# Forming gated-unit and gate projections of a conformer block from seven block products instead of eight

## The chip, the cores and the metric

The kernel runs on one core of a Trainium2 chip. Of its engines TensorE (PE) multiplies matrices, VectorE (DVE), ScalarE (ACT) and GpSimd (POOL) work elementwise, and SyncE (SP) issues nearly all transfers. The metric is the device time of one execution in microseconds. Three executions of the kernel before took 1762.32 to 1763.79 us, with a median of 1763.37 us.

## The reference

One block over 1024 tokens of width 1024 in float32: a gated convolution branch and an attention branch, mixed by gates, then a feed-forward part with a short convolution. Cut to what matters here:

```
h = rms_norm(x, norm1_g)
z = h @ w_in
glu_in, q, k, v, gate_logits = split(z)

a = a_val * sigmoid(a_gate)                       # glu_in: 1024 + 1024 channels
a = causal_depthwise_conv(a, conv_w, conv_b)      # 31 taps for each channel
a = silu(rms_norm(a, conv_norm_g))
y_a = a @ w_conv_out

o = mix of three dilated causal window attentions over q, k, v (16 heads)
y_b = o @ w_attn_out

g = sigmoid(gate_logits + gate_b)                 # 1024 + 1024 channels
g_a, g_b = split(g)
x = x + (g_a * y_a + g_b * y_b) @ w_out

u = causal_depthwise_conv(rms_norm(x, norm2_g) @ w_up, ffn_conv_w, ffn_conv_b)   # 3 taps
x = x + (silu(u_gate) * u_val) @ w_down
```

The kernel merges the three attentions into one with a host-made mask for each head.

## The kernel before

**Numbers.** Every operand of a large matmul is split into a high and a low part (`split`, L76: ACT copies the high part into a rounded format, DVE subtracts it from the source), and a product is three matmuls: high by high, high by low, low by high. One matmul takes a 128x128 piece of weights or activations against 512 columns. A weight block of 128 output channels and 1024 inputs is a `[128, 1024]` tile: `stage` (L81) loads it into `raw`, and `wsplit` (L86) splits it into `whi` and `wlo`. Each of these three has four buffers.

**The order of the work.** The program is written as loops, and a planner orders each engine's instructions at build time by program order and by a timeline that it computes. Inside the `manual_schedule` blocks the order on ACT, DVE and PE is as written. The stages are:

1. *Start.* Eight token tiles of x are normalised and transposed into `hT`, which is high and low parts for token halves 0 and 1. The first gated-unit pair, channel block 0 of `a_val` with block 0 of `a_gate`, is computed in between (`first_pair`, L338).
2. *Gated units.* The other seven pairs: for each, 96 matmuls over the two weight blocks and the two token halves (`gemm_ch`, L115), a sigmoid on ACT and a product on DVE (L445) into `apad`, the convolution's input, which stays on the chip (ten buffers, used for the results too).
3. *Projections of q, k and v.* Six column groups by eight token tiles of 24 matmuls each (`gemm_tok`, L120). ACT and DVE normalise, transpose (on PE) and split the results, which go out to DRAM.
4. *The convolution* (`conv_branch`, L450) is 31 instructions on DVE for each of eight channel blocks (L458, L461), then squares on ACT and their sum on DVE (L469). It stands behind stage 3 in the program, and so it takes the time on DVE that stages 2 and 3 leave. PE sums the squares over channels (`pss`, L553), POOL takes the power, and PE spreads it over partitions (`psr`, L563). Then eight products on DVE (L568), silu on ACT (L569) and a transfer to DRAM (`da`, L570) end it.
5. *Side work.* `side_steps` (L178) is a generator of 48 uses of eight steps. A step is three matmuls of a gate projection (16 channel blocks by two token halves) or of `w_conv_out` (eight by two). `cover` (L542) takes `COVER[0]` = 24 steps ahead of `pss`, 8 steps between it and `psr`, and 20 steps behind the eight products. The last four gate blocks also ask for the convolution's results.
6. *Attention*, in a written order of 128 slots, eight a head (L654). In a slot PE computes scores for 128 queries (`score`, L581), DVE adds the mask and finds the minimum (L592), ACT takes the exponential, DVE and POOL normalise, and `BACK` = 5 slots later PE turns the result (`flip`, L603, matmuls of L607), ACT and DVE split it, and PE multiplies it by the values. `fill` (L639) takes `FILL[slot % 8]` steps of the side work in each slot, 17.5 a head. Attention's tiles lie on the memory of the convolution.
7. *The rest*: the gates are applied, `w_out`, the up projection and the down projection. Both of the last are already formed from seven block products; for the up projection `product` (L846), `up_sums` (L872) and `up_rest` (L1028) do it, and the token blocks for it are formed in `blocks`.

The lines that decide how the side work is spread:

```
FILL = (1.5, 3.4, 1.8, 1.9, 1.6, 3.0, 2.1, 2.2)
BACK = 5
SHARE = 0.6
COVER = (24, 8, 20)
```

Of the kernel before, what the change touches and what calls it, by code (L numbers as in the profile page):

```python
# [21 lines left out]
P = 128  # L22
# [12 lines left out]
FILL = (1.5, 3.4, 1.8, 1.9, 1.6, 3.0, 2.1, 2.2)  # L35
BACK = 5
SHARE = 0.6
COVER = (24, 8, 20)
# [14 lines left out]
def block_kernel(ctx: ExitStack, tc: tile.TileContext, x, g1, g2, pack, mask,  # L53
# [50 lines left out]

    def gemm_half(o, w, actT, half):

        hi, lo = w
        ah, al = actT[0][half], actT[1][half]
        for k in range(KT):
            pe.matmul(o, hi[:, k, :], ah[:, k, :], start=(k == 0), stop=False)  # L110
            pe.matmul(o, hi[:, k, :], al[:, k, :], start=False, stop=False)  # L111
            pe.matmul(o, lo[:, k, :], ah[:, k, :], start=False, stop=(k == KT - 1))  # L112
            yield

    def gemm_ch(ps, w, actT):  # L115
        for half in range(2):
            for _ in gemm_half(ps[:, half * 512 : half * 512 + 512], w, actT, half):
                pass

    def gemm_tok(ps, actT, wpieces, tt):  # L120

        half, c0 = tt // 4, (tt % 4) * P
        for k in range(KT):
            hi, lo = wpieces[k // 2]
            ah = actT[0][half][:, k, c0 : c0 + P]
            al = actT[1][half][:, k, c0 : c0 + P]
# [15 lines left out]
    da = dr.tile([P, KT, T], F32, name="da")  # L142
    dya = [dr.tile([P, T], F32, name=f"dya{i}") for i in range(8)]
# [34 lines left out]
    def side_steps(hT, da):  # L178
# [18 lines left out]
        def gate(c, half):  # L197
            def go(w):
                gp = bank_ps(f"gate_{c}_{half}")
                if c >= 12 and half == 1:  # L200
                    if not aT:
                        aT.extend(hb_tiles(hb1, "aT"))
                    ask_conv(0, 2 * (c - 12))
# [25 lines left out]
        for c in range(12):  # L229
            for half in range(2):  # L230
                gate(c, half)
        for half in range(2):
            for c in range(12, 16):
                gate(c, half)
        for c0 in (0, 4):
# [8 lines left out]
        for i, (_, n, go) in enumerate(uses):  # L244
# [7 lines left out]
            if n.startswith("co"):  # L252
                need = max(need, marks[(i - 32) // 4 % 2])
# [23 lines left out]
    p1a_cm = tc.tile_pool(name="ph1a", bufs=1, side="right")  # L277
    p1a = p1a_cm.__enter__()
    with tc.tile_pool(name="ph1", bufs=1) as p1:
        t4 = lambda name, dt=F32: p1a.tile([P, 1024], dt, tag="t4", bufs=4, name=name)  # L280
        g1r = p1.tile([1, D], F32, tag="csq", bufs=1, name="g1r")
        act.dma_start(g1r, g1.unsqueeze(0))
        xt = []
        for tt in range(8):
            xx = p1.tile([P, CW - 1 + T], F32, tag="apad", bufs=10, name=f"x_{tt}")[:, 0:T]
            sp.dma_start(xx, x[tt * P : (tt + 1) * P, :])
            xt.append(xx)
            if tt == 3:
                wfirst = [(c, n, stage(w_ch[c], n)) for c, n in ((8, "g0"), (0, "v0"))]
# [5 lines left out]
        hT = hb_tiles(hb1, "hT")  # L295

        glu0 = [big_ps("glugv_0"), None]
        third = big_ps("tp_2")
        gb1 = p1.tile([P, D], F32, tag="sqacc", bufs=1, name="gb1")
        xn = [t4(f"xs_{tt}") for tt in range(4)]  # L300
        st1 = p1.tile([P, 2, 8], F32, name="st1")
        tps = {}

        def squares(tt):
            if tt >= 4:
                xn.append(t4(f"xs_{tt}"))
# [9 lines left out]
        def turned(tt):  # L316
            for kk in range(2):
                ps = third[:, kk * 512 : kk * 512 + 512] if tt == 2 else bank_ps(f"tp_{tt}_{kk}")
# [5 lines left out]
        def part(tt, kk, a):  # L324
            half, c0 = tt // 4, (tt % 4) * P
            return hT[a][half][:, kk * 4 : kk * 4 + 4, c0 : c0 + P]
# [11 lines left out]
        def first_pair(half, ks, passes, which):  # L338
            o = glu0[half][:, which * 512 : which * 512 + 512]
            for wa, ha in passes:  # L340
                for k in ks:
                    pe.matmul(o, wfirst[which][wa][:, k, :], hT[ha][half][:, k, :],
                              start=(k == 0 and (wa, ha) == (0, 0)), stop=(k == 7 and (wa, ha) == (1, 0)))

        ENG = mybir.EngineType
        HH, HL, LH = ((0, 0),), ((0, 1),), ((1, 0),)
        with tc.manual_schedule(engines={ENG.Activation, ENG.DVE, ENG.PE}):
# [9 lines left out]
            for tt in range(4):  # L357
# [4 lines left out]
                if tt == 2:  # L362
# [4 lines left out]
            hl = [[wp.tile([P, 1024], F32R, tag=t, bufs=4, name=f"{t}_{n}") for t in ("whi", "wlo")]  # L367
                  for _, n, _ in wfirst]
            wraw = [r for _, _, r in wfirst]
            wfirst = [[t.rearrange("p (a b) -> p a b", a=KT) for t in w] for w in hl]  # L370
# [30 lines left out]
            squares(7)  # L401
            both(4, 0)
            scaled(6)
            spread1(7)
            both(5, 0)
            turned(6)
            both(4, 1)
            scaled(7)
            both(5, 1)
            first_pair(0, b, HL, 1)  # L410
            turned(7)
            first_pair(0, b, LH, 1)
            both(6, 0)
            both(7, 0)
            glu0[1] = big_ps("glugv_1")
            both(6, 1)
            ends = both(7, 1)
        for ks in (a, b):
            for which in range(2):
                first_pair(1, ks, HH + HL + LH, which)  # L420
        with tc.issue_after(ends[1].ins):
            dve.tensor_tensor(out=qkg, in0=pk[:, C_QG : C_QG + 1], in1=pk[:, C_KG : C_KG + 1], op=ALU.mult)
            dve.tensor_scalar(qkg, qkg, DH ** -0.5, None, op0=ALU.mult)
        with tc.issue_after(ends[0].ins), tc.issue_after(ends[1].ins):
            wsecond = [wpiece(w_ch[9], "g1"), wpiece(w_ch[1], "v1")]


        apad = []
        for c in range(8):
            a = p1.tile([P, CW - 1 + T], F32, tag="apad", bufs=10, name=f"apad_{c}")  # L430
            pool.memset(a[:, : CW - 1], 0.0)
            sg = t4(f"sg_{c}")
            if c == 0:
# [848 lines left out]
```

## Time and profile before

| what | value |
| --- | --- |
| median of three executions | 1763.37 us |
| profiled execution: span from first to last instruction | 1761.6 us |
| PE busy | 1749.1 us, 99% of the span |
| DVE busy | 1329.3 us, 75% |
| ACT busy | 771.7 us, 44% |
| moved by DMA | 272.79 MB, mean 155 GB/s |

The profiled execution has no time of its own beside its span; the span is 1.8 us under the median. A row of a group names the line, the engine, the operation, what is written and read, shapes and count, then its busy time and the mean duration of one. A mean duration counts the time in the pipeline, so that neighbours overlap; where a price is wanted, the distance from one start to the next is read. A row of the timeline or of the chain of waits begins with the start and the duration in us.

### The profile page before, as it was taken

How to read it: one execution, taken by the hardware profiler on the slowest of the kernel's cores; microseconds unless marked ns; L12 is line 12 of the kernel's file. 1: busy time of each engine (PE TensorE's matmuls, PEld its weight loads, DVE VectorE, ACT ScalarE, POOL GpSimd, SP SyncE). 2: the span in 40 equal slices, each digit the busy share in tenths (PEclk: the TensorE clock that was granted, in tenths of full speed). 3: DMA queues.
4: the chain of work that ended last, by engine and by line, in shares of the span. 5: the costliest groups of instructions: out<-in, count | busy, mean ns of one | idle time of the engine just before them, and what ended most of it. 6: DMA issues, size and time to landing. Idle time of an engine off the chain costs nothing.

```text
span 1761.6 us, 22662 instructions
## 1 busy us (share of the span) xinstructions
PE 1749.1 (99%) x8248; PEld 1454.3 (83%) x8248; DVE 1329.3 (75%) x1837; ACT 771.7 (44%) x1235; POOL 185.9 (11%) x193
## 2 busy tenths in 40 slices
PE   8999999999999999999999999999999999999999
PEld 6888888888888888888888888888888888888887
DVE  6999999999846666667655564687776777779863
ACT  6111132232256666667564343454544544534431
POOL 1000133034012222222210000000000000000000
PEclk9999999999999999999999999999999999999999
DMA  5111145344585655568446567532222222498851
GB/s 208 48 48 49 42 138 164 123 132 139 179 273 157 179 159 159 161 180 244 139 138 227 173 233 279 207 124 84 84 84 84 77 91 84 128 341 320 292 174 48
DMA packets 146530, 272.79 MB, mean 155 GB/s; under 512 B 11761, under 2 KB 61041, under 8 KB 146418
## 3 DMA queue, kind: packets, MB, share of 16 engines
q1 hardware_dynamic: 145264, 269.24, 47.2%
q10 hardware_dynamic: 1154, 2.10, 0.3%
q8 instruction: 65, 1.06, 0.2%
q14 instruction: 47, 0.39, 0.1%
HBM read 197.90 MB, written 73.40 MB: 154 GB/s over the span
## 4 chain that ended last, share of the span: by engine, by line
PE 93%; DMA 4%; DVE 1%; issue 1%; ACT 1%; SPq 0%; ACTq 0%; DVEq 0%
PE dx L1118 6%; PE xz L850 6%; PE xz L851 6%; PE xz L852 6%; PE qkv L129 5%; PE qkv L127 5%; PE qkv L128 5%; PE dy L1118 4%; PE pp L607 3%; PE gate L110 3%; PE gate L112 3%; PE gate L111 3%; PE y L850 2%; PE y L851 2%; PE y L852 2%; PE o L622 2%
## 5 line engine op out<-in xcount | busy, mean ns | idle before, releaser
L461 DVE SCALAR_TENSOR_TENSOR cacc<-apad,pk,cacc 128x1024 f32<-128x1024 f32 x240 | 299.7, 1288 | 0.7
L79 DVE TENSOR_TENSOR pl<-pp,ph 128x512 fp32r<-128x512 f32 x192 | 100.8, 553 | 88.1 <-ACT ph L78 87.9
L127 PE MATMUL qkv<-hi_qkv,hT 128*128 128x512 f32 x384 | 151.8, 396 | 0.0
L129 PE MATMUL qkv<-hi_qkv,hT 128*128 128x512 f32 x384 | 150.2, 391 | 0.0
L128 PE MATMUL qkv<-lo_qkv,hT 128*128 128x512 f32 x384 | 149.3, 389 | 0.0
L78 ACT ACTIVATE ph<-pp 128x512 fp32r<-128x512 f32 x192 | 87.1, 488 | 121.0 <-PE pp L607 120.3
L592 DVE CUSTOM_DVE_ANT_0 p<-s,m 128x128 f32<-128x128 f32 (+7 forms) x128 | 96.5, 754 | 53.3 <-PE s L588 41.4
L601 POOL TENSOR_SCALAR p<-p,st 128x128 f32<-128x128 f32 (+7 forms) x128 | 97.1, 758 | 315.7 <-DVE st L600 218.7
L1021 DVE SCALAR_TENSOR_TENSOR u<-u,pk 128x1023 f32<-128x1023 f32 x88 | 112.4, 1279 | 1.0 <-ACT u L1019 0.7
L103 POOL TENSOR_TENSOR rs<-ss,mhalf 128x8 f32<-128x8 f32 x32 | 75.0, 2348 | 337.6 <-DVE ss L102 337.6
L110 PE MATMUL gate<-hT,hi_gt 128*128 128x512 f32 x256 | 103.0, 402 | 0.0
L597 ACT ACTIVATE p<-p,st 128x128 f32<-128x128 f32 (+7 forms) x128 | 99.3, 775 | 5.5 <-DVE st L592 4.6
L111 PE MATMUL gate<-hT,hi_gt 128*128 128x512 f32 x256 | 100.3, 392 | 0.0
L112 PE MATMUL gate<-hT,lo_gt 128*128 128x512 f32 x256 | 100.1, 392 | 0.0
L129 PEld LDWEIGHTS qkv<-hi_qkv,hT 128*128 128x128 f32 x384 | 72.1, 188 | 15.3
L79 DVE TENSOR_TENSOR lo_uv<-raw_uv,hi_uv 128x1024 fp32r<-128x1024 f32 x20 | 24.5, 1226 | 79.5 <-ACT hi_uv L78 79.5
L128 PEld LDWEIGHTS qkv<-lo_qkv,hT 128*128 128x128 f32 x384 | 72.2, 188 | 14.3
L607 PE MATMUL pp<-ident,p 128*128 128x128 f32 x576 | 83.8, 272 | 0.0
L127 PEld LDWEIGHTS qkv<-hi_qkv,hT 128*128 128x128 f32 x384 | 72.2, 188 | 13.9
L607 PEld LDWEIGHTS pp<-ident,p 128*128 128x128 f32 x576 | 70.1, 140 | 15.3
L621 PE MATMUL o<-ph,v 128*128 128x512 f32 x192 | 74.8, 393 | 0.7 <-DVE op L633 0.7
L850 PE MATMUL xz<-blk_t,hi_s3g 128*128 128x512 f32 x176 | 68.6, 390 | 0.7 <-ACT xc L995 0.7
(309 smaller groups left out, 4638.8 us busy)
## 6 DMA issues: line engine op xcount, KB each, us to landing
wr<-w_down SPq DMA_DIRECT2D x45, 512.0 KB, 5.5
gr<-dff SPq DMA_DIRECT2D x62, 256.0 KB, 5.2
raw_qkv<-w_qkv SPq DMA_DIRECT2D x24, 512.0 KB, 3.8
dff<-u SPq DMA_DIRECT2D x22, 512.0 KB, 2.6
raw_uv<-w_up SPq DMA_DIRECT2D x21, 512.0 KB, 3.2
raw_ug<-w_up SPq DMA_DIRECT2D x20, 512.0 KB, 3.2
dv<-v SPq DMA_DIRECT2D x16, 512.0 KB, 3.2
raw_gt<-w_ch SPq DMA_DIRECT2D x16, 512.0 KB, 5.2
```

The source lines that it names most:

```text
L110: pe.matmul(o, hi[:, k, :], ah[:, k, :], start=(k == 0), stop=False)
L111: pe.matmul(o, hi[:, k, :], al[:, k, :], start=False, stop=False)
L112: pe.matmul(o, lo[:, k, :], ah[:, k, :], start=False, stop=(k == KT - 1))
L127: pe.matmul(ps, ah, hi[:, k % 2, :], start=(k == 0), stop=False)
L128: pe.matmul(ps, ah, lo[:, k % 2, :], start=False, stop=False)
L129: pe.matmul(ps, al, hi[:, k % 2, :], start=False, stop=(k == KT - 1))
L461: dve.scalar_tensor_tensor(out=acc, in0=a[:, j : j + T], scalar=w(j), in1=acc, op0=ALU.mult, op1=ALU.add)
L607: pe.transpose(pp[:, qb * P : (qb + 1) * P], pts[qb][:, kt * P : (kt + 1) * P], ident)
L850: pe.matmul(o, wh[:, k, :], bh[:, k, :], start=(start and k == 0), stop=False, skip_group_check=not start)
L851: pe.matmul(o, wh[:, k, :], bl[:, k, :], start=False, stop=False, skip_group_check=not start)
L852: end = pe.matmul(o, wl[:, k, :], bh[:, k, :], start=False, stop=(k == 3), skip_group_check=not start)
L1118: pe.matmul(banks[n], a[:, c], b[:, d], start=(start and i == 0 and m == 0), stop=(stop and i == nf - 1 and m == 2), skip_group_check=True)
```

## The change

For a pair of weight blocks, call the halves of the first a11, a12 (inputs 0 to 511, 512 to 1023) and those of the second a21, a22, and call the blocks of the activations b11, b21 (token half 0) and b12, b22 (token half 1). The two outputs for two token halves are eight block products of 12 matmuls. The change forms them from seven, with these sums:

```
s1 = a21 + a22   s2 = s1 - a11   s3 = a11 - a21   s4 = a12 - s2
t1 = b12 - b11   t2 = b22 - b12 + b11   t3 = b22 - b12   t4 = b21 - t2
```

- Pairs 0 and 1 of the gated unit stay plain and are computed at the start, half by half (`first_pair`). Their results go to DRAM (`dain`).
- Behind them DVE and ACT form and split t1 to t4, each 128 x 2048. They lie in a pool `phT` that lives until the last pair; b12 is parked in DRAM (`db12`) and fetched again, because its memory holds the pairs' outputs (`uring`).
- Pairs 2 to 7 of the gated unit, then gate blocks 0 and 1 with their partners 8 and 9, come from seven products (`pair_weights`, `pair_first`, `pair_sums`, `pair_rest`). The gated units go to DRAM, the gate logits too.
- The convolution reads its input from DRAM into two `apad` buffers. Its results stay on the chip: channel blocks 1 and 2 in two `cacc` buffers, 0 (by way of DRAM) and 3 to 7 in a pool `phc`, which lies behind `ph1`.
- The side work has 40 uses (12 gate blocks by two halves, then `w_conv_out`). `COVER[0]` is 48, and `FILL` is 12.4 steps a head.

The diff, cut:

```diff
-FILL = (1.5, 3.4, 1.8, 1.9, 1.6, 3.0, 2.1, 2.2)
+FILL = (1.1, 2.4, 1.3, 1.35, 1.15, 2.1, 1.5, 1.5)
-COVER = (24, 8, 20)
+COVER = (48, 8, 20)
+GATES = 2
+FAR = 3
...
-        for c in range(12):
+        left_over = [c for c in range(16) if c % 8 >= GATES]
+        turn = left_over[-4:]
+        for c in left_over[:-4]:
             for half in range(2):
                 gate(c, half)
...
+        def differ(tt):
+            c = slice((tt % 4) * P, (tt % 4) * P + P)
+            if "t1" not in plain:
+                plain["t1"] = p0.tile([P, 4, 512], F32, tag="xa", name="t1_sum")
+            act.activation(plain["t1"][:, :, c], tps[tt, 0], AF.Copy)
+            dve.tensor_tensor(out=plain["t3"][:, :, c], in0=tps[tt, 1], in1=plain["t1"][:, :, c], op=ALU.subtract)
...
+        pairs = [("u", c, w_ch[c], w_ch[8 + c]) for c in range(2, 8)]
+        pairs += [("t", c, w_ch[16 + c], w_ch[24 + c]) for c in range(GATES)]
...
+        def pair_first(xz, w):
+            for i, o in enumerate(xz):
+                b = [h0[a][:, 4 * i : 4 * i + 4] for a in range(2)]
+                product(o, four(w[0])[:, 4 * i : 4 * i + 4], four(w[1])[:, 4 * i : 4 * i + 4], *b, True)
...
+        def pair_sums(i, v):
...
+            add_(s1, a21, a22, ALU.add)
+            add_(s2, s1, a11, ALU.subtract)
+            sw = wsplit(s, f"{n}s12_{c}")
+            add_(a21, a11, a21, ALU.subtract)
+            gw = wsplit(g, f"{n}s3g_{c}")
+            add_(a12, a12, s2, ALU.subtract)
+            return [four(t) for t in sw], [four(t) for t in gw], [four(t) for t in wsplit(a12, f"{n}s4_{c}")]
...
+        spill(db12, upper[0])
+
+        def glu_end(c, half):
+            sg = cst.tile([P, 512], F32, tag="f2", bufs=2, name=f"sg_{c}_{half}")
+            act.activation(sg, glu[c, half][:, 0:512], AF.Sigmoid)
+            dve.tensor_tensor(out=sg, in0=glu[c, half][:, 512:1024], in1=sg, op=ALU.mult)
+            sp.dma_start(dain[c][:, half * 512 : half * 512 + 512], sg)
...
+        def form(n):
+            forms[n] = tform(n)
+            split(forms[n][:, 0], forms[n][:, 1], plain[n])
+
+        for n, k in (("t2", 0), ("t4", 4)):
+            dve.tensor_tensor(out=plain[n], in0=h0[0][:, k : k + 4].bitcast(F32),
+                              in1=h0[1][:, k : k + 4].bitcast(F32), op=add)
+        dve.tensor_tensor(out=plain["t1"], in0=plain["t1"], in1=plain["t2"], op=sub)
+        form("t1")
+        dve.tensor_tensor(out=plain["t2"], in0=plain["t3"], in1=plain["t2"], op=add)
+        form("t3")
+        form("t2")
+        dve.tensor_tensor(out=plain["t4"], in0=plain["t4"], in1=plain["t2"], op=sub)
+        form("t4")
...
+            put(uv[:, t0], X, 0)
+            dve.tensor_tensor(out=uv[:, t0], in0=Z, in1=uv[:, t0], op=add)
+            product(X, sh[:, 4:8], sl[:, 4:8], *fb["t2"], False)
+            put(uv[:, t1], X, 0)
+            product(Y, sh[:, 0:4], sl[:, 0:4], *fb["t1"], True)
+            put(p5, Y, 1)
+            product(X, gh[:, 0:4], gl[:, 0:4], *fb["t3"], False)
+            dve.tensor_tensor(out=ug[:, t1], in0=X, in1=p5, op=add)
+            product(Y, *s4, *fb["b22"], False)
+            dve.tensor_tensor(out=uv[:, t1], in0=Y, in1=uv[:, t1], op=add)
+            product(X, gh[:, 4:8], gl[:, 4:8], *fb["t4"], False)
+            put(ug[:, t0], X, 1)
+            if kind == "u":
+                act.activation(ug, ug, AF.Sigmoid)
+                dve.tensor_tensor(out=uv, in0=uv, in1=ug, op=ALU.mult)
+                sp.dma_start(dain[c], uv)
...
+        upper[0] = hb1.tile([P, 2, 4, 512], F32R, tag="hb01", name="b12_again")
+        fetch(upper[0], db12)
...
+                a = p1.tile([P, CW - 1 + T], F32, tag="apad", bufs=2, name=f"apad_{c}")
+                pool.memset(a[:, : CW - 1], 0.0)
+                sp.dma_start(a[:, CW - 1 :], dain[c])
+                if c < FAR:
+                    acc = p1.tile([P, T], F32, tag="cacc", bufs=2, name=f"cacc_{c}")
+                else:
+                    acc = pc.tile([P, T], F32, name=f"cn_{c}")
...
+                if c < FAR - 2:
+                    sp.dma_start(dacc[c], acc)
+                    acc = pc.tile([P, T], F32, name=f"cn_{c}")
+                    sp.dma_start(acc, dacc[c])
+                cn.append(acc)
```

More of the change, by code (lines that the diff above doesn't have):

```diff
@@ L410, in block_kernel @@
-            first_pair(0, b, HL, 1)
+            differ(5)
             turned(7)
-            first_pair(0, b, LH, 1)
+            glu[1, 0] = big_ps("glugv_10")
+            for which in range(2):
+                first_pair(0, (*a, *b), HH + HL + LH, which, 1)
             both(6, 0)
             both(7, 0)
-            glu0[1] = big_ps("glugv_1")
             both(6, 1)
[L417 to L420, printed above, removed]
```

236 lines of the change are left out of this document (153 added, 83 removed).

## The prediction

> **What bounds the kernel now.** I read the page first (busy shares, then the 40 slices), then the chain of waits, then windows and timelines round the place where the convolution ends.
>
> ```profile
> span 1761.6 us, 22662 instructions
> PE 1749.1 (99%) x8248; PEld 1454.3 (83%) x8248; DVE 1329.3 (75%) x1837; ACT 771.7 (44%) x1235; POOL 185.9 (11%) x193
> ...
> PE   8999999999999999999999999999999999999999
> ...
> DVE  6999999999846666667655564687776777779863
> ...
> PEclk9999999999999999999999999999999999999999
> ...
> L461 DVE SCALAR_TENSOR_TENSOR cacc<-apad,pk,cacc 128x1024 f32<-128x1024 f32 x240 | 299.7, 1288 | 0.7
> ```
>
> PE is busy in every slice, at the full granted clock: the end is set by the number of matmuls, so fewer of them is worth something. But the DVE row is also full, from slice 2 to slice 10 (44 to 440 us). What fills it is the convolution of L461, 300 us of work that yields to everything else. So in the first 480 us two engines are full, and a change that unloads the one and loads the other has to be counted on both.
>
> The price of a matmul is not its 390 ns mean but its distance to the next, which the chain of waits shows; the last two rows are the same point of two neighbouring column blocks of the up projection, which already forms a pair from seven products:
>
> ```profile
> 1719.91 5.44 PE dy L1118 x24
> ...
> 1299.07 0.45 PE xz L852 x2
> 1318.11 0.45 PE xz L852 x2
> ```
>
> 5.44 / 24 = 0.2267 us; 84 matmuls a pair times 0.2267 is 19.04, which is what the two rows are apart. A seven-product pair costs PE its matmuls and no wait there.
>
> The two ends of the convolution stage, PE's rows first, then DVE's, then the windows (columns: busy us of PE, PEld, DVE, ACT, POOL; clock; DMA):
>
> ```profile
> 470.45 0.39 PE L110 MATMUL gate<-hT,hi_gt 128*128 128x512 f32 x1
> ...
> 486.77 1.84 PE L553 MATMUL pss<-ones,sqacc 128*128 128x1 f32 x16
> ...
> 521.21 0.60 PE L607 MATMUL pp<-ident,p 128*128 128x128 f32 x4
> ```
>
> ```profile
> 480.61 1.23 DVE L469 TENSOR_TENSOR sqacc<-sqacc,csq 128x1024 f32<-128x1024 f32 x1 [1.19 <-ACT csq L468]
> ...
> 497.23 9.17 DVE L568 TENSOR_TENSOR cacc<-cacc,sqacc 128x1024 f32<-128x1024 f32 x8
> 513.06 0.29 DVE L592 CUSTOM_DVE_ANT_0 p<-s,m 128x128 f32<-128x128 f32 x1 [6.66 <-DMA da<-cacc]
> ```
>
> ```profile
> 0.00:44.00 44.00, 38.44 (x175) 30.07 (x176) 30.35 (x45) 26.77 (x42) 6.95 (x24) 1.00 0.55 209
> 44.00:482.00 438.00, 438.00 (x1994) 362.36 (x1993) 425.60 (x448) 102.54 (x140) 75.02 (x32) 1.00 0.34 106
> 482.00:513.00 31.00, 30.86 (x154) 25.81 (x152) 14.79 (x23) 14.71 (x18) 1.64 (x1) 1.00 1.03 315
> ...
> 550.00:600.00 50.00, 50.00 (x276) 42.62 (x276) 32.60 (x82) 30.80 (x71) 12.24 (x17) 1.00 0.56 158
> ```
>
> The last addition of squares ends at 481.84. PE left the projections at 470.45, covers with 24 gate steps (24 x 3 x 0.2267 = 16.3 us) and asks for the sum at 486.77: DVE is 5 us early. From there to the first flip of attention (521.21) PE has gate steps to do. The balance is a matter of 5 us; this is the place to watch.
>
> **The change, part by part.**
>
> *Matmuls.* Eight pairs go from 96 to 84: 96 fewer, 96 x 0.2267 = 21.8 us of PE. Nothing else on PE changes in number. Without any new idle time: 1763.4 - 21.8 = 1741.6 (span 1761.6, so 1.8 us lie around it). This is the floor.
>
> *DVE work ahead of the convolution's end.* Prices from DVE's timeline of the up projection, as distances between starts:
>
> ```profile
> 1313.90 1.22 DVE L79 TENSOR_TENSOR lo_s3g<-raw_ug,hi_s3g 128x1024 fp32r<-128x1024 f32 x1
> 1315.03 1.22 DVE L1025 TENSOR_TENSOR u<-u 128x1024 f32<-128x1024 f32 x1
> 1316.16 0.69 DVE L877 TENSOR_TENSOR s<-raw_ug 128x512 f32<-128x512 f32 x1
> 1316.77 1.28 DVE L1021 SCALAR_TENSOR_TENSOR u<-u,pk 128x1023 f32<-128x1023 f32 x1
> ```
>
> 1.13 us for 1024 columns, 0.60 for 512. A 2048-column addition is not in the trace: 1.13 + 2 x 0.53 = 2.2 at least, four times 0.60 = 2.4 at most; I take 2.2, since the step from 512 to 1024 shows the fixed part paid once.
> - A gated-unit pair: low halves of three 1024-wide weights and one 512 (3 x 1.13 + 0.60), four weight sums (2.4), three block sums (1.8), the gating product (1.13): 9.3. Before: two low halves and the product, 3.4. Six pairs: +35.6.
> - A gate pair: the same without the product, 8.2. Two: +16.4. The splits that they take out of the gate steps lay behind, since 48 cover steps ask for five weights where 24 asked for four: +1.2.
> - Token blocks: five additions and four low halves of 2048 columns, 9 x 2.2 = 19.8, and four 512-wide differences, 2.4: +22.2.
> - The two plain pairs cost what pairs 0 and 1 cost before.
>
> Together +75.4 us. The convolution cannot end before all of it is done, because it takes what DVE has left. DVE had 30.35 + 425.60 = 456.0 us busy and 26 idle up to 482; now 531.4 busy. Of the 26, some 15 belong to the first loads and to waits that a later filler cannot use; all 26 and 3 more (the first conv input now goes out to DRAM and back) is the other end. End of the convolution: 546 to 560; I take 553, the middle, as the idle rows do not say which of them go.
>
> *PE up to the first flip.* 521.2, plus 21.8 (96 more matmuls stand ahead of the projections: 192 + 8 x 84 against 768), plus 16.3 (24 more cover steps), less 2.0 (the first five slots fill 7.3 steps instead of 10.2): 557.3 if PE never waits. So DVE gets 71 us later and PE 36.
>
> *From the conv's end to the first flip.* Before: 34.4 us from the sum (486.77) to the flip (521.21), which PE filled; inside it the eight products end at 506.4, 19.6 after the sum, and the first score row waits 6.66 us for a normalised conv tile to leave, since it lies on that memory. Now the results lie in a pool of their own and the buffers that the convolution frees at its end come first in memory, where the early score tiles fall. The bounds: 12 (scores go into the gaps ahead of the products; the copies are done 10.5 after the sum) and 34.4. I take 18, nearer to the end of the products, since attention's first five slots need no flip and two score tiles in PSUM are all PE can run ahead. First flip 553 + 18 = 571; PE idle 571 - 557.3 = 14.
>
> The Trainium skill, "TensorE: Matmul & The Clock Gate", Part 1 (the HAM clock gate), says that after an idle window of about 3.4 us PE falls to half its clock and needs as long to come back. By that an idle stretch of 14 us would add up to about 1.7 us, an estimate from that page. This trace cannot settle it: its granted clock is full in all 40 slices, and it has no idle stretch so long.
>
> *Hidden parts.* ACT's extra casts and copies: ACT is busy 102.54 of 438 us in that window. The conv inputs through DRAM (8 x 0.5 MB out and in), the parked block (2 MB each way) and one result (0.5 MB each way) are 13.6 MB, 27 GB/s over 500 us at a DMA share of 0.34; SP's queue waits for the parked block behind the last pair's writes, but it is wanted only by the fifth token tile, 4 x 24 x 0.2267 = 21.8 us into the projections. Without that cover its 2 MB at the 315 GB/s of the 482 to 513 window cost 7 us. A wait inside the pair stage (a low half behind a conv instruction, 1.28 each) costs nothing while PE would idle later anyway; else 8 x 1.28 = 10 us. I take 0.5.
>
> *Attention with less fill.* Two heads, by the chain:
>
> ```profile
> 531.94 0.87 PE pp L607 x8
> ...
> 581.60 0.87 PE pp L607 x8
> ```
>
> 49.66 us. Fill falls from 17.5 to 12.4 steps a head, so 5.1 x 0.68 = 3.5 us a head go elsewhere: 42.7 for two. DVE has 32.60 and ACT 30.80 busy per 50 us, so 76% and 72% of the shorter time; with five slots between score and flip I expect little waiting: 0 to 10 us, I take 2 (nearest to the present rows, where PE is busy 50.00 of 50).
>
> Sum: 1763.4 - 21.8 + 14 + 2 + 0.5 = **1758** us.
>
> **The rivals.**
> - *Nearly all of the gain stays.* The conv ends at 546 and the scores slip in at 12: flip at 558, idle 1. 1763.4 - 21.8 + 1 + 1 = 1744. For it: DVE's idle time is waste that a longer queue could use. Against: it needs both low ends.
> - *DVE takes it all back (slower).* Place: PE's wait for the conv's sum and the tail behind it. If the conv ends at 556 or later and the tail stays as it is (34.4), the flip comes at 590: idle 33, 1763.4 - 21.8 + 33 + 1 = 1776. It decides from a first flip at 557.3 + 21.8 = 579 on. For it: +71 against +36 is the firmest count here, and the present tail is a measured row. Against: part of the tail was PE's own steps.
> - *Attention starves.* If a head cannot go below 23 us where PE needs 21.4, 16 x 1.6 = 26 us come on top of the idle 14: about 1782. DVE at 76% with in-order queues speaks for it, the five slots against.
> - *It doesn't do what it says*: pairs that wait as above, on a PE that is not idle later: 1763.4 - 21.8 + 10 + 3 = 1755, no longer apart from the forecast.
>
> **How the numbers follow.** Forecast (1749 to 1766) 0.45, of it 0.25 below and 0.20 within the 0.2% (3.5 us: 1759.8 to 1766.9) that a measurement of this kernel can tell from no change; nearly all stays 0.22; DVE takes it back 0.26; starving 0.07. The pair-wait case lies inside the first. Faster 0.25 + 0.22 = 0.47, same 0.20, slower 0.33. The range, 1744 to 1779, reaches from the first rival's number to just past the second's, leaving out the starving case and the ends. The forecast's own range is 1749 to 1766.
>
> **What would show it.** Pairs about 19.04 us apart between the plain pairs and the projections: the matmul part is right. DVE busy about 531 us up to the last addition of squares, and that addition between 546 and 560: the DVE count is right. PE's idle time gathered in one or two gaps between 525 and 575, released by the conv's sum, by a score tile or by a conv result's DMA: the idle term; its size against 14 decides between forecast and rivals. Heads 21.4 us apart: attention is not starved. The forecast is wrong if PE shows no idle stretch of over 5 us there, or one of over 25.

## The result, and the profile after

The kernel after takes 1783.34 us (median of 4 executions, 1780.02 to 1784.36) against 1763.58 us before (1762.32 to 1763.86): a ratio of 1.0109, 95% interval 1.0095 to 1.0123. It is slower by 1.1%, where 1758 was forecast, and 4 us above the top of the range. The rival "DVE takes it all back" is what happened.

The page, the rows that answer to those of before:

```profile
span 1781.2 us, 22699 instructions
PE 1740.7 (98%) x8152; PEld 1442.4 (81%) x8152; DVE 1394.6 (78%) x1919; ACT 809.0 (45%) x1280; POOL 185.5 (10%) x193
...
PE   7999999999996999999999999999999999999999
...
DVE  8999999999996677787764564687777777779863
...
PEclk9999999999998999999999999999999999999999
...
L628 DVE SCALAR_TENSOR_TENSOR cn<-apad,pk,cn 128x1024 f32<-128x1024 f32 x150 | 188.5, 1285 | 0.3
```

PE executes 8152 matmuls instead of 8248: the 96 are gone. But its row has a 6 in slice 13 (534 to 579 us), and its clock an 8 there. DVE's full stretch now ends two slices later than before. The waits of PE, longest first, say what PE stood for there:

```profile
PE pss L723 <- DVE sqacc L635: 14.5, 1, 14.5
PE qt L666 <- DVE qn L658: 5.5, 2, 4.2
PE tp L353 <- DVE sums L379: 2.8, 1, 2.8
```

And windows of the same kernel, of which the first overlaps the others (columns: length; busy us and instructions of PE, PEld, DVE, ACT, POOL; clock; DMA share; GB/s):

```profile
0.00:559.00 559.00, 527.36 (x2359) 431.29 (x2359) 533.66 (x588) 181.22 (x252) 79.64 (x56) 0.98 0.44 144
...
0.00:44.00 44.00, 34.35 (x142) 25.66 (x143) 35.40 (x50) 27.21 (x44) 7.30 (x16) 0.96 0.58 225
44.00:219.00 175.00, 174.08 (x767) 143.54 (x766) 167.33 (x168) 65.41 (x79) 0.30 (x3) 1.00 0.28 95
219.00:260.00 41.00, 36.78 (x156) 30.10 (x156) 39.32 (x43) 7.06 (x11) 9.69 (x5) 0.92 0.46 167
...
544.00:559.00 15.00, 0.50 (x5) 0.32 (x3) 13.46 (x12) 2.78 (x4) 0.00 (x0) 0.68 0.18 62
559.00:594.00 35.00, 34.69 (x156) 29.18 (x157) 16.06 (x34) 16.76 (x24) 3.78 (x5) 0.89 0.41 153
594.00:963.00 369.00, 366.90 (x2036) 311.47 (x2035) 262.03 (x647) 254.14 (x556) 96.85 (x124) 1.00 0.63 180
```

From 44 to 219 us, where the pairs are, PE works 174.08 of 175 us: the pairs themselves hardly wait. From 544 to 559 it does next to nothing (0.50 us), while DVE, busy 13.46 of 15, finishes the convolution. Then it works without a pause up to the first flip, 34.69 of 35 us, but at a clock of 0.89. These are the two ends of the stage, PE's timeline and DVE's:

```profile
544.17 0.28 PE L758 MATMUL s<-kl,q 128*128 128x128 f32 x1
558.95 3.58 PE L723 MATMUL pss<-ones,sqacc 128*128 128x1 f32 x16 [14.50 <-DVE sqacc L635]
562.38 0.77 PE L116 MATMUL gate<-hT,hi_gt 128*128 128x512 f32 x1
...
566.37 0.40 PE L116 MATMUL gate<-hT,hi_gt 128*128 128x512 f32 x1
...
569.81 1.31 PE L733 MATMUL psr<-dg,ones 128*128 128x128 f32 x10
```

```profile
557.67 1.23 DVE L635 TENSOR_TENSOR sqacc<-sqacc,apad 128x1024 f32<-128x1024 f32 x1 [1.18 <-ACT apad L634]
...
576.16 0.69 DVE L735 COPY sqacc<-psr 128x512 f32<-128x512 f32 x1 [4.37 <-PE psr L733]
576.88 1.23 DVE L738 TENSOR_TENSOR cn<-cn,sqacc 128x1024 f32<-128x1024 f32 x1
...
580.30 5.76 DVE L738 TENSOR_TENSOR cn<-cn,sqacc 128x1024 f32<-128x1024 f32 x5
585.97 0.29 DVE L762 CUSTOM_DVE_ANT_0 p<-s,m 128x128 f32<-128x128 f32 x1
```

The last addition of squares ends at 558.90 (before: 481.84), 77.1 us later. The first flip comes in the chain of waits of this kernel as follows, and two rows of the same form two heads apart stand behind it:

```profile
593.95 0.44 PE pp L777 x4
...
645.80 0.92 PE pp L777 x8
...
689.18 0.87 PE pp L777 x8
```

(PE's first flip starts at 593.8, 72.6 us later than before.) Behind it two heads take 43.38 us; before, 49.66. So up to the first flip the kernel loses 72.6 us, and behind it it gains 53.0, which is the fill moved forward and not a gain in work; the span is 19.6 longer.

### The profile page after: what moved, and what is told of

It is laid out like the page before. It is cut to its first block, busy times and chain, and to the rows that moved or that the text cites. A ratio compares the mean times of both kernels' runs of the same rounds, so it can differ in the third digit from the quotient of the medians.

```text
span 1781.2 us, 22699 instructions
## 1 busy us (share of the span) xinstructions
PE 1740.7 (98%) x8152; PEld 1442.4 (81%) x8152; DVE 1394.6 (78%) x1919; ACT 809.0 (45%) x1280; POOL 185.5 (10%) x193
## 4 chain that ended last, share of the span: by engine, by line
PE 88%; DVE 7%; ACT 2%; DMA 1%; issue 1%; POOL 0%; SPq 0%; DVEq 0%; ACTq 0%; POOLq 0%
PE dx L1278 6%; PE xz L124 6%; PE xz L126 6%; PE xz L125 6%; PE dy L1278 5%; PE qkv L140 3%; PE qkv L139 3%; PE qkv L141 3%; PE pp L777 3%; DVE cn L628 3%; PE gate L116 2%; PE y L126 2%; PE y L125 2%; PE y L124 2%; PE gate L117 2%; PE gate L118 2%
## 5 line engine op out<-in xcount | busy, mean ns | idle before, releaser
L628 DVE SCALAR_TENSOR_TENSOR cn<-apad,pk,cn 128x1024 f32<-128x1024 f32 x150 | 188.5, 1285 | 0.3
L762 DVE CUSTOM_DVE_ANT_0 p<-s,m 128x128 f32<-128x128 f32 (+7 forms) x128 | 96.4, 753 | 27.5 <-PE s L758 19.6
L628 DVE SCALAR_TENSOR_TENSOR cacc<-apad,pk,cacc 128x1024 f32<-128x1024 f32 x90 | 113.9, 1284 | 0.2
L81 DVE TENSOR_TENSOR lo_uv<-raw_uv,hi_uv 128x1024 fp32r<-128x1024 f32 x26 | 31.9, 1226 | 81.0 <-ACT hi_uv L80 80.4
L140 PE MATMUL qkv<-lo_qkv,hT 128*128 128x512 f32 x192 | 74.8, 391 | 0.9 <-DVE lo_qkv L81 0.9
L141 PE MATMUL qkv<-hi_qkv,hT 128*128 128x512 f32 x192 | 75.0, 391 | 0.0
L139 PE MATMUL qkv<-hi_qkv,hT 128*128 128x512 f32 x192 | 74.7, 395 | 0.0
L124 PE MATMUL xz<-blk_t,hi_s3g 128*128 128x512 f32 x176 | 68.6, 390 | 0.7 <-ACT xc L1155 0.7
L124 PE MATMUL xz<-h2left,hi_uv 128*128 128x512 f32 x176 | 68.6, 390 | 0.0
L125 PE MATMUL xz<-blk_t,hi_s3g 128*128 128x512 f32 x176 | 68.5, 389 | 0.0
L126 PE MATMUL xz<-h2left,lo_uv 128*128 128x512 f32 x176 | 68.5, 389 | 0.0
L125 PE MATMUL xz<-h2left,hi_uv 128*128 128x512 f32 x176 | 68.5, 389 | 0.0
L126 PE MATMUL xz<-blk_t,lo_s3g 128*128 128x512 f32 x176 | 68.5, 389 | 0.0
```

What stands on the lines that cost most here:

```text
L81: dve.tensor_tensor(out=lo, in0=src, in1=hi.bitcast(F32), op=ALU.subtract)
L124: pe.matmul(o, wh[:, k, :], bh[:, k, :], start=(start and k == 0), stop=False, skip_group_check=not start)
L125: pe.matmul(o, wh[:, k, :], bl[:, k, :], start=False, stop=False, skip_group_check=not start)
L126: end = pe.matmul(o, wl[:, k, :], bh[:, k, :], start=False, stop=(k == 3), skip_group_check=not start)
L628: dve.scalar_tensor_tensor(out=acc, in0=a[:, j : j + T], scalar=w(j), in1=acc, op0=ALU.mult, op1=ALU.add)
```

## The experiments

The theory after the result: the time follows the end of the convolution on DVE one to one, and what PE saves or loses ahead of it counts for nothing (A). The rivals: PE's own losses ahead of the reduction (B), the slots of work behind the reduction, attention, or the placing of a few additions. "Flip" is the first `pp`; all in us:

| run | median | ratio to before, 95% interval | last add ends | PE waits there | flip | median less last add |
| --- | --- | --- | --- | --- | --- | --- |
| before | 1763.58 | | 481.8 | 0 | 521.2 | 1281.7 |
| after | 1783.34 | 1.0095 to 1.0123 | 558.9 | 14.5 | 593.8 | 1224.4 |
| tap30 | 1775.45 | 1.0048 to 1.0078 | 551.0 | 11.9 | 585.8 | 1224.5 |
| start | 1780.86 | 1.0080 to 1.0114 | 555.6 | 20.5 | 590.6 | 1225.3 |
| tail | 1864.03 | 1.0546 to 1.0578 | 644.1 | 102.7 | 675.3 | 1219.9 |
| tail2 | 1778.76 | 1.0076 to 1.0106 | 556.5 | 9.1 | 588.4 | 1222.3 |
| cover80 | 1774.89 | 1.0045 to 1.0075 | 562.1 | 0 | 597.8 | 1212.8 |
| pool | 1789.82 | 1.0137 to 1.0167 | 563.1 | 7.9 | 599.0 | 1226.7 |
| pool_start | 1787.17 | 1.0122 to 1.0156 | 561.7 | 6.6 | 597.3 | 1225.5 |
| gates0 | 1779.55 | 1.0076 to 1.0106 | 548.3 | 4.8 | 583.4 | 1231.3 |
| best8 | 1772.96 | 1.0036 to 1.0064 | 557.4 | 6.1 | 594.1 | 1215.6 |
| best6 | 1766.86 | 1.0013 to 1.0031 | 547.2 | 0 | 582.9 | 1219.7 |
| before33 | 1780.75 | 1.0083 to 1.0111 | 501.0 | 7.9 | 538.9 | 1279.8 |
| tap25 | 1757.77 | 0.9958 to 0.9979 | 485.6 | 0 | 566.4 | |

Each ratio is to the kernel before as it was measured beside that run (medians 1762.96 to 1764.46). The intervals of start, tail2 and gates0 overlap with that of after, so their gains of 2.5 to 4.6 us are not clear of the spread by time alone; the other columns, but for the last, are read from one profiled execution each.

**One tap less.** The convolution sums 30 taps instead of 31; the last one is left out.

```diff
-                for j in range(CW):
+                for j in range(30):
```

> Edit: the convolution leaves out its last tap in each of the eight channel blocks (30 instead of 31; that part of the computation is missing). VectorE gets 8 x 1.2 = 9.6 us less to do ahead of the sum of squares, and no other engine changes. Theory A (VectorE's queue ahead of the convolution's end sets when attention starts, and TensorE waits for it): the last addition of squares moves from 558.9 to about 549, TensorE's wait for it shrinks from 14.8 to about 5 us, and the time falls by the whole 9.6, to 1771 to 1775. Rival B (what TensorE loses by itself ahead of the projections' end, about 19 us in the start, in the clock and at the first projection tiles, is the price): no change, 1781 to 1785.

Measured: last add 7.9 us earlier (9.6 were expected), time 7.9 us less (the table's last column stays the same to 0.1). The time follows DVE one to one.

**PE's losses ahead of the reduction.** The sums that DVE does for the first pairs are held back until the token blocks' differences are done (`settled0` is the last of these), and the differences are taken one step earlier.

```diff
+            differ(4)
+            differ(5)
...
-            add_(s1, a21, a22, ALU.add)
-            add_(s2, s1, a11, ALU.subtract)
+            with tc.issue_after(settled0.ins):
+                add_(s1, a21, a22, ALU.add)
+                add_(s2, s1, a11, ALU.subtract)
```

> Edit: in the start, the sums for t2 and t4 and the small gain product may not go ahead of the last difference on VectorE, and the differences of tiles 4 and 5 go ahead of the second weight pair's split. TensorE should lose some 5 of the 7.5 us that the start has lost, VectorE's total work stays. Rival B: the time falls by 4 to 6, to 1777 to 1779. Theory A: TensorE only reaches the wait for the sum of squares earlier and waits longer there (18 to 20 us instead of 14.8); the time stays, 1781 to 1785.

Measured: PE comes to the reduction at 534.9 instead of 544.2, 9.3 us earlier, and waits there 20.5 us instead of 14.5. The time falls by 2.5 us, about what the last add moved (3.3). PE's early losses were hidden behind DVE; B falls.

**More cover ahead of the reduction.** The cover is 80 steps instead of 48, taken from attention's fill (10.4 steps a head instead of 12.4).

```diff
-FILL = (1.1, 2.4, 1.3, 1.35, 1.15, 2.1, 1.5, 1.5)
-COVER = (48, 8, 20)
+FILL = (0.92, 2.01, 1.09, 1.13, 0.96, 1.76, 1.26, 1.26)
+COVER = (80, 8, 20)
```

> Edit: 80 cover steps ahead of the sum instead of 48, and fill in attention lowered from 12.4 to 10.4 steps a head, so that 32 steps (21.8 us of TensorE) move ahead of the convolution's end. Theory A: the wait of 14.8 us is filled, and the slow clock behind it does not come; the first flip stays near 594; 1764 to 1768. Rival C (attention with less fill is held up by VectorE and ScalarE, so that steps moved out of it do not shorten it): the time falls by less than 8, 1775 or more. Rival B: the wait goes, but the 19 us lost earlier stay; it says the same as A here.

Measured: 8.4 us less, not the 15 or more expected. The wait is gone, but the last add ends 3.2 us later, since two of the cover's low halves (1.29 us) and a wait of 1.78 us for ACT's high half stand in DVE's queue ahead of it, and PE comes to it 4.5 us after it. The flip is 4.0 us later. Behind the flip the time falls by 12.4 us only, where the 32 steps that moved are 21.8. The same window of cover80 and of after:

```profile
598.00:956.00 358.00, 350.67 (x1945) 294.24 (x1944) 257.57 (x643) 249.88 (x549) 96.22 (x124) 1.00 0.65 182
```

```profile
598.00:956.00 358.00, 355.90 (x1984) 302.28 (x1983) 254.63 (x637) 247.41 (x547) 95.36 (x123) 1.00 0.63 177
```

PE idles 358 - 350.67 = 7.3 us instead of 2.1: 3.9 us for POOL's part of the softmax (after: 1.7) and 2.5 us for DVE's and ACT's splits of the turned results. With ten fill steps a head attention begins to starve; its 5.2 us more are part of the 9.4 that are missing, and where the rest goes is not shown. Cover and fill come out of one store.

**The tail.** The 8 steps between the two reductions go ahead of them, and the diagonal tiles have eight buffers instead of four. (The kernel before has eight as well, L561; the change took four of them away, L731.)

```diff
-COVER = (48, 8, 20)
+COVER = (56, 0, 20)
...
-            dg = p1.tile([P, P], F32, tag="dg", bufs=4, name=f"dg_{tt}")
+            dg = p1.tile([P, P], F32, tag="dg", bufs=8, name=f"dg_{tt}")
```

> Edit: the eight cover steps between the sum over channels and its spreading go ahead of the sum (56, 0, 20), and the eight diagonal tiles have eight buffers instead of four. Theory A: the spreading is done 4 to 8 us earlier behind the sum, the score tiles and the first flip too, and the time falls by as much, to 1775 to 1780. If the tail's length is set by the products, the silu and the transfers alone, nothing changes (1782 to 1785). Rival B: no change.

Measured: 80.7 us more, which no theory expected. DVE's timeline of this run, the convolution's first instructions:

```profile
229.43 1.23 DVE L81 TENSOR_TENSOR lo_qkv<-raw_qkv,hi_qkv 128x1024 fp32r<-128x1024 f32 x1 [8.11 <-ACT hi_qkv L80]
230.58 0.81 DVE L625 TENSOR_SCALAR cacc<-apad,pk 128x1024 f32<-128x1024 f32 x1
231.42 1.28 DVE L628 SCALAR_TENSOR_TENSOR cacc<-apad,pk,cacc 128x1024 f32<-128x1024 f32 x1
```

and of after:

```profile
68.24 0.81 DVE L625 TENSOR_SCALAR cacc<-apad,pk 128x1024 f32<-128x1024 f32 x1 [1.29 <-DMA apad<-dain]
69.09 1.28 DVE L628 SCALAR_TENSOR_TENSOR cacc<-apad,pk,cacc 128x1024 f32<-128x1024 f32 x1
```

It starts 162 us later, after the pairs, and its first input is fetched at 221.45 instead of 64.97. That the four buffers do it is shown by the next run, which leaves them out. How is not shown. They are 2 KB a partition in the pool that holds the convolution's buffers too, and may shift these onto memory that the pairs still use. As a test of A the accident is a good one: the last add comes 85.2 us later and the time grows by 80.7.

**The tail without the buffers.**

```diff
-COVER = (48, 8, 20)
+COVER = (56, 0, 20)
```

> Edit: the eight cover steps between the sum over channels and its spreading go ahead of the sum (56, 0, 20); the diagonal tiles keep their four buffers, so the memory is laid out as in the changed kernel. Theory A: the convolution starts and ends as in the changed kernel (first at 69, sum at 559), the spreading ends 4 to 5 us sooner and the time falls by that, to 1778 to 1780. If the tail hangs on products, silu and transfers alone: 1782 to 1785.

Measured: 4.6 us less. The last add comes 2.4 us earlier, and from it to the flip it is 31.9 instead of 34.9. The 8 steps that left PE's queue there are 5.4 us at the normal distance; 2.4 us of this come back as a wait of `psr` for the diagonal tiles (`dg`).

**The sums on GpSimd.** The four weight sums of a pair move from DVE to GpSimd, to unload DVE.

```diff
-            add_ = lambda o, a, b, op: dve.tensor_tensor(out=o, in0=a, in1=b, op=op)
+            add_ = lambda o, a, b, op: pool.tensor_tensor(out=o, in0=a, in1=b, op=op)
```

> Edit: the four weight sums of each of the eight pairs (512 columns each) move from VectorE to GpSimd. VectorE loses 8 x 4 x 0.60 = 19 us ahead of the convolution's end. Theory A: the last addition of squares goes from 558.9 to about 540, TensorE (there at 544) no longer waits, the first flip comes at 575 to 580 and the time falls by 14 to 19, to 1764 to 1769. If GpSimd's slower sums hold the pairs up, or slow VectorE down, the addition comes later than 545 and the gain is under 10. Rival B: at most the 3 us of the slow clock behind the wait.

> Edit: the start's reordering and the sums on GpSimd together. Theory A: with the start alone TensorE reached the wait 9 us earlier for nothing; now that VectorE is 19 us less busy that is worth something: the addition at about 537, TensorE there at about 535, the time 1759 to 1764, some 4 under the sums on GpSimd alone. Rival B: the start alone would have shown it; no difference between the two.

Measured: 1789.82 us, and with the order of the run start 1787.17 (1.0122 to 1.0156, last add 561.7): slower than after, the opposite of what was expected. Groups of DVE's instructions between 70 and 240 us, of after and of pool, and then GpSimd's of pool:

```profile
L628 DVE SCALAR_TENSOR_TENSOR cacc<-apad,pk,cacc 128x1024 f32<-128x1024 f32 x72 | 90.9, 1285 | 0.2
...
L81 DVE TENSOR_TENSOR lo_us<-raw_uv,hi_us 128x512 fp32r<-128x512 f32 x6 | 4.2, 698 | 0.3 <-ACT hi_us L80 0.3
```

```profile
L628 DVE SCALAR_TENSOR_TENSOR cacc<-apad,pk,cacc 128x1024 f32<-128x1024 f32 x74 | 111.2, 1527 | 0.1
L81 DVE TENSOR_TENSOR lo_us<-raw_uv,hi_us 128x512 fp32r<-128x512 f32 x6 | 8.4, 1405 | 0.0
```

```profile
L410 POOL TENSOR_TENSOR us<-raw_ug 128x512 f32<-128x512 f32 x5 | 12.6, 2526 | 46.6 <-DVE lo_us3g L81 28.4 <-DMA raw_ug<-w_ch 18.2
...
L410 POOL TENSOR_TENSOR raw_uv<-raw_uv,us 128x512 f32<-128x512 f32 x5 | 9.2, 1842 | 24.2 <-DVE lo_uv L81 24.2
```

A sum takes GpSimd 1.8 to 2.5 us in the mean where DVE takes 0.69, and DVE's own instructions stretch: the conv's from 1285 to 1527 ns in the mean, a low half from 698 to 1405. The unloading costs DVE more than it takes off: without the sums it is busy for 538.8 us up to its last add, with them 533.7. The Trainium skill, "SBUF — State Buffer", section "SBUF: two separate sides", says that VectorE, with two inputs in SBUF, and GpSimd take turns on one pair of ports, and that the later one stands still for the whole instruction of the other; the stretched rows agree. Besides, PE now waits in the pairs, 5.2 us for a low half (`lo_uv`) at the longest, and the projections begin at 236.4 instead of 219.3.

**Without the two gate pairs.** Gate blocks 0, 1, 8 and 9 are formed plainly again (24 matmuls or 5.4 us more), and these steps go to the cover.

```diff
-FILL = (1.1, 2.4, 1.3, 1.35, 1.15, 2.1, 1.5, 1.5)
-COVER = (48, 8, 20)
-GATES = 2
+FILL = (1.14, 2.5, 1.35, 1.4, 1.2, 2.18, 1.56, 1.56)
+COVER = (104, 8, 20)
+GATES = 0
```

> Edit: no gate pairs (GATES 0): only the six gated-unit pairs come from seven products. TensorE has 24 matmuls more (5.4 us); VectorE has 16.4 less ahead of the convolution's end. The gates' steps go back into the side work: 104 cover steps instead of 48 and 12.9 fill steps a head, so that TensorE reaches the wait at about 544 as before. Theory A: the addition at about 542, flip near 577, time 1768 to 1773, so the two gate pairs cost more than they bring. Theory that counts TensorE alone: 1783 + 5 = 1788.

Measured: 3.8 us less than after, with more matmuls, though not the 10 or more expected. The last add ends 10.6 us earlier and the flip 10.4; behind the flip 6.6 of it are lost again, 5.4 of them for the eight steps more that are left there (8 x 0.68). By the medians the two gate pairs were a net loss, and by the last add they cost DVE more (10.6 us) than they took from PE (5.4).

**The pieces together.** best8 has the order of start, `COVER = (72, 0, 30)` and 10.75 fill steps a head; best6 has no gate pairs, the order of start, `COVER = (120, 0, 26)` and 12.0 steps.

```diff
-FILL = (1.1, 2.4, 1.3, 1.35, 1.15, 2.1, 1.5, 1.5)
-COVER = (48, 8, 20)
-GATES = 2
+FILL = (1.06, 2.32, 1.26, 1.31, 1.11, 2.03, 1.45, 1.45)
+COVER = (120, 0, 26)
+GATES = 0
```

> The kernel after with three edits together: the sums of the first pairs are held back as in the run named start, 72 of conv's cover steps instead of 56 stand ahead of its reduction (and 30 instead of 20 behind it), and the heads' fill is 10.75 steps each instead of 11.5. Theory A (the time follows the end of the conv's last add and what stands on TensorE's queue until the first flip): the last add ends near 556 us as in the run start; TensorE reaches the reduction near 550, so that some 5 us of the 20.8 us wait of start stay; flip near 591 with ten more steps done ahead of it, and 10 steps (6.8 us) fewer among the heads: 1780.9 minus 6.8 minus what the tail saves, 1760 to 1775 by what attention pays for the missing fill. Theory B (attention is starved by fewer fill steps, as cover80 began to show with 7.3 us of idle TensorE): 1775 or above, and TensorE idle 10 us or more between flip and the last head.

> Six pairs from seven products, the two gate pairs plain as before the change (24 more matmuls than after, 5.4 us), with the sums held back as in start and 120 cover steps ahead of the reduction, 26 behind it, fill 12.0. Theory A: conv's last add near 545 us (548.3 in gates0 minus the 3 us of start), TensorE at the reduction at about the same moment with a wait under 5 us, flip near 582, time 1763 to 1772. Theory B (attention starves or the pairs stall): 1776 or above.

Measured: 1772.96 and 1766.86 us. In best6 PE comes to the reduction 1.7 us after the last add, so neither engine waits for the other there, and it still is 0.22% slower than before. The waits of PE in best6:

```profile
PE qt L670 <- DVE qn L662: 4.8, 2, 3.0
PE tp L353 <- DVE xs L340: 2.8, 2, 2.2
PE psr L737 <- DVE dg L736: 2.4, 1, 2.4
PE gb L426 <- DMA gb<-g: 2.3, 1, 2.3
PE qkv L139 <- DMA b_again<-db: 2.1, 1, 2.1
```

With DVE's excess covered PE's own waits count, the parked block's among them; which of them make the 2.8 us is not shown. In best8 the greatest wait behind the flip is 6.1 us of `pp` for POOL's share of the softmax (10 times): the sign of starving that theory B named, below the time it gave.

**How near was the kernel before?** The kernel before, with the last two taps done twice in each channel block (16 DVE instructions more, about 19 us; the result is that of another convolution).

```diff
-                for j in range(CW):
+                for j in (*range(CW), CW - 2, CW - 1):
```

> The kernel before with the conv's last two taps done twice in each channel block (33 VectorE instructions instead of 31 by block, so this kernel does more work than before and computes another conv). It asks how close the kernel before stood to this bound: TensorE waited 5 us for the conv there. Theory A (conv's end sets the first flip already before): the last add goes from 481.8 to about 499 us, the wait at the reduction from 5 to 18 us or so, and the time from 1763 to 1776 to 1782. Theory B (the kernel before had slack that the change used up only in part): time within 3 us of before.

Measured: 1780.75, 16.7 us more than the 1764.08 of the kernel before beside it. PE's row of this run:

```profile
PE pss L553 <- DVE sqacc L469: 7.9, 1, 7.9
```

The last add comes 19.2 us later and the flip 17.7. In the kernel before DVE was 4.9 us early at the reduction (481.84 against 486.77; the expectation says that PE waited those 5 us, which is the wrong way round). These were to spare: 19.2 - 4.9 = 14.3. The other 3.4 us of the flip's 17.7 are a longer tail, 37.8 us instead of 34.4, with PE at a clock of 0.88 behind its wait. So the kernel before stood 5 us from this bound.

**DVE out of the way.** The order of start, with 25 taps instead of 31 (six are left out).

```diff
-                for j in range(CW):
+                for j in range(25):
```

> The kernel of the run named start with six of the 31 taps left out in each channel block (the conv's output is another for it): 48 VectorE instructions, some 58 us, fewer ahead of the conv's end. It asks what the change would be worth if VectorE did not set the end, so what TensorE itself lost in pairs, projections and attention. Theory A (only VectorE's lateness and the slots behind it are in the way): the conv's last add ends near 500 us or somewhat later, TensorE comes to the reduction at 534 to 536 without a wait, the first flip comes at 560 to 570, and the time is 1750 to 1760. Theory B (pairs and attention give the gain back as well, so that a free VectorE does not bring it): no wait at the reduction, but 1765 or above, with TensorE's idle time in other rows, between 219 and 511 us or behind the flip.

Measured: 1757.77 us, 23.1 less than start. The last add ends at 485.6, 49 us ahead of PE, which does not wait. Its windows:

```profile
486.00:535.00 49.00, 49.00 (x220) 40.58 (x218) 10.44 (x16) 12.73 (x22) 0.00 (x0) 1.00 0.74 220
535.00:566.00 31.00, 30.69 (x156) 25.78 (x155) 16.74 (x36) 17.92 (x26) 3.49 (x5) 1.00 0.52 192
```

From `pss`, which starts at 534.8, to the flip it is still 31.6 us here, with the sum done long before: PE is busy for all but 0.3 us of it, so the tail is PE's own queue.

So what the change is worth with a free DVE is 5.9 us (0.3%), not 21.8. (The kernel before has all its taps in this comparison. Its PE is 99% busy, so fewer would hardly help it; no run shows it.) The other 15 or so (span 1754.8 against 1761.6 - 21.8 = 1739.8) are PE's: the flip comes at 566.4, 9.1 after the 557.3 of a PE that never waits; from there to the first `yb` 369.6 us pass, 4.3 more than the fill moved forward accounts for (88 steps fewer stand behind the covers, 2.9 of them ahead of the flip: 423.2 - 85.1 x 0.68 = 365.3); and 1.6 behind that.

## Why the prediction was wrong

*The steps that held.* The matmuls: 96 fewer, and PE 99% busy in the pair stage. The DVE count: 531.4 us up to the last add were worked out, 533.66 are in the window to 559. The conv's end: 546 to 560 was the range, 558.9 the result; the middle was taken, and the upper end was right. Of the 5.9 us beyond the 553 taken 2.3 are busy time and 3.6 idle time: 25 us of idle DVE stayed.

*The step that failed: the tail from the conv's end to the first flip, taken as 18 us, measured 34.9* (before: 34.4). The prediction looked at DVE and at memory there, and that part of the mechanism came true: before, the first `p` waited 6.66 us for a conv result to leave, and after it waits for nothing. But it took nothing off the tail, because PE has no time to spare in it. Behind `pss` PE's queue holds 28 cover steps and some 8 of fill (108 matmuls, 36 x 0.68 = 24.5 us), `psr` and the first scores. The prediction's own sums have this work: its PE reaches the reduction at 486.8 + 21.8 + 16.3 = 524.9 and the flip at 557.3, 32.4 us apart. It let PE do part of it while PE waits for the sum, and even named these steps as a reason for a shorter tail. PE did 0.50 us of work from 544 to 559 and all the rest behind the sum, busy 34.69 of 35 us. Two runs bear this out: in tap25, with the sum ready 49 us early, the tail is 31.6; in tail2, with 8 steps moved ahead of `pss`, it is 3.0 shorter. So from its own rows the flip was to be looked for at 553 + 32.4 = 585, not at 571.

In pieces, before and after: from the sum to the start of `psr` 7.4 and 10.9, since PE comes out of its idle stretch at a low clock with eight steps in its queue; from there to the products 3.0 and 7.1, since with four diagonal tiles instead of eight the second half of `psr` waits for the first and then stands behind cover steps; the products 9.2 and 9.1; the wait for memory 6.7 and 0; from `p` to the flip 8.1 and 7.8. One wait of 6.7 went, and 7.6 us came on PE's queue. PE had the first score done at 544, and still the mask row `p<-s,m` starts at 585.97, right behind the last of the eight products (580.30 + 5.76): on DVE the products stand first. Whether a mask row ahead of them would have helped is not shown, but the second score runs at 585.96 only, behind the cover steps on PE. The bounds of the prediction, 12 and 34.4, were too narrow by a little and the choice between them was wrong.

With it the sum comes out: flip 593.8 instead of 571, 22.8 us, of which 16.9 are the tail and 5.9 the conv's end. The 2.5 us that are then left to 1783.3 lie behind the flip, beyond the 2 + 0.5 taken.

*"PE up to the first flip: 557.3 if it never waits"* failed too, without a price. PE came to the reduction at 544.2, where that count has 524.9: 19.3 us late. Up to there it idled some 17 us, where the kernel before has 5.6 up to 486.77: in the start (142 matmuls by 44 us; before 175), and 4.2 us at 246 us, where `qt` waits for DVE's `qn`. The rest is in part the lower clock there (0.96 in the first 44 us, 0.92 from 219 to 260). The parked block came late as well: its fetch is issued at 237.9 and takes 7.9 us, so that the cover of 21.8 us from 219.3 on was not whole; but PE still had other work until 246.6, and no wait in this kernel is put down to it. The run start shows that PE's lateness was hidden; in best6 and tap25, with DVE out of the way, what is left of it counts, and in best6 2.1 us of it are a wait for the parked block.

*The forecast needed PE to idle 14 us; the wait of 14.5 at the reduction looks like it and is not.* That the two agree is chance: the wait is short because PE came 19.3 us late, and the run start makes it 20.5 by bringing PE earlier. The prediction named the size of this idle time as what decides between the forecast and its rivals, and so its own sign would have pointed to the forecast. Measured against 557.3 the flip is 36.5 late: 19.3 before PE reaches the reduction, 14.7 of wait, 2.5 behind it. The rival had 33.

*The clock.* The rows say: after 14.5 us of idle PE's `pss` takes 3.58 us instead of 1.84, and the nine distances between matmuls from 562.38 to 566.37 are 0.443 us in the mean where 0.2267 is normal: together 1.7 + 1.9 = 3.7 us, at a clock of 0.89 in that window, while before had full clock in all slices. The prediction quoted a rule on this from the Trainium skill ("TensorE: Matmul & The Clock Gate", Part 1). The trace agrees with its half rate (0.443 is 1.95 times 0.2267), but not with its length: the slow stretch lasted 7.4 us here, not about 3.4, and so it cost 3.7 us where the estimate was 1.7.

*The rivals.* "DVE takes it all back" had its place, its point of decision (579; measured 593.8) and its tail right, and gave 1776; its flip was 3.4 us early, and the rest of what it lacks lies behind the flip. Its tail was a row of the kernel before, where the forecast's was a choice between bounds. "Nearly all stays" was refuted even with a free DVE: tap25 keeps 5.9 of 21.8. "Attention starves" did not come at 12.4 steps a head (43.38 us for two heads, 42.7 worked out), and begins at 10.4 to 10.75. "Pairs that wait": not in the pairs, but in the projections behind them.

## What to carry to other kernels

Where two engines end a stage within a few microseconds of each other, price a change on both and set the later of the two ends against the time: here a gated-unit pair took 2.7 us from PE and put 5.9 on DVE, with 22 us once for the token blocks, and while DVE was the later one the time followed it one to one. Work that stands on an engine's queue behind the thing it waits for is added to the wait, so count it from there; that a wait of another engine goes away is worth nothing as long as this queue is full. Work used as a cover can be spent once: moved ahead of a reduction, it is missing in the stage that it came from.

## What the runs showed of the hardware

- Additions on GpSimd (1.8 to 2.5 us in the mean for 512 columns, run pool) stretch DVE's instructions beside them; a low half took 1405 ns in the mean instead of 698.
- PE's clock in the kernel after was 0.68 in a window of 15 us with hardly any work and 0.89 in the 35 us after it, and 0.92 round a wait of 4.2 us. Behind the wait of 14.5 us matmuls were 0.443 us apart instead of 0.2267, and the slow stretch lasted 7.4 us. In cover80 and tap25, where PE does not wait at the reduction, the clock behind it is 1.00.
- A 2048-column addition on DVE, bounded from 2.2 to 2.4 in the prediction, is 2.2 us from start to start (44.10 to 46.30 us in the kernel after).
